# Reordering which activations stay on the chip, when gates and activations are requested, and how gathered rows are spread over the last stages of a layer on Trainium2

## The chip, the cores and the metric

The kernel runs on one core of a Trainium2 chip. The metric is device microseconds of one execution, the median of several runs. Engines are named as in the profile: PE (matrix multiplies; PEld is its weight load), DVE (vector), ACT (scalar), POOL, and SP, which only issues transfers. Transfers are issued from SP, ACT and POOL and run on 16 shared DMA engines. Everything is float32; each matrix product is done as three products of a high and a low part (hi*hi, hi*lo, lo*hi).

## The reference, cut to what matters

One layer for 512 tokens of width 2048: a mixer of two attention-like branches, a cross attention to 256 memory rows, and an expert layer, each followed by a layer norm over a scaled residual. The change lies in the expert layer.

```python
def reference(x, mem, w_in, ...):
    h = hybrid_mixer(x, w_in[l], ...)
    x = layer_norm(DN_ALPHA * x + h, ln_w[l, 0], ln_b[l, 0])
    h = memory_cross_attention(x, mem, w_xq[l], w_xkv[l], w_xo[l])
    x = layer_norm(DN_ALPHA * x + h, ln_w[l, 1], ln_b[l, 1])
    h = peer_ffn(x, peer_wq[l], peer_sub_keys[l], peer_u[l], peer_v[l])
    x = layer_norm(DN_ALPHA * x + h, ln_w[l, 2], ln_b[l, 2])

def peer_ffn(x, w_pq, sub_keys, expert_u, expert_v):   # 8 heads, 128 x 128 = 16384 experts
    q = (x @ w_pq).reshape(B, S, PEER_HEADS, 2, PEER_DK // 2)
    sc = jnp.einsum('bshpd,hpnd->bshpn', q, sub_keys)
    top_s, top_i = lax.top_k(sc, PEER_TOPK)             # 16 of 128, twice per head
    ...                                                  # 16 of the 256 pairs per head
    idx = jnp.take_along_axis(cand_i, best_pos, -1)
    g = jax.nn.softmax(best_s, -1)
    ...                                                  # per block of 128 tokens, 128 experts a token:
        u = expert_u[it]
        a = jnp.einsum('tkd,td->tk', u, xt)
        hact = jax.nn.gelu(a, approximate=False) * gt
        return jnp.einsum('tk,tkd->td', hact, expert_v[it])
```

## The kernel before

**Two ways through the expert layer.** Tokens 0 to 255 (two blocks of 128) fetch the experts that they chose: for each of the 128 choices of a block, one indirect transfer from POOL brings 128 rows of 2048 floats (1 MB, tile `rows`, three buffers) of `peer_u`, later of `peer_v`; DVE takes one pass over each (L1041 a dot product, L1057 a multiply and add). Tokens 256 to 511 use all 16384 experts: U and V are streamed whole, and a table of gates, zero where an expert is not chosen, is multiplied in. The table and the streams are cut by *keys*: key c (0 to 127) is a group of 128 experts.

**How a streamed megabyte is used.** `load_raw` asks for 1 MB on SP's queue (tile `raw`). `shares` has ACT copy it to the high part (L179, two instructions of 128x1024) and DVE subtract to get the low part (L182) in one of two `ring` tiles; PE multiplies from the ring. At each share the function `tick` is called.

**`tick` hands out the gathered rows.** `set_rate(980.0)` makes the rate 256/980 rows a unit for the 256 rows (128 of U, then 128 of V) of token block 1. Each tick adds rate * cost * `state["mult"]` to a credit that is cut at 2.0; each whole credit issues one gather, and DVE's pass over it is put two ticks later. A share of `peer_wq` or V costs 4.0 units, one of U 4.2. `state["mult"]` is set anew for each stage. All 256 must be handed out shortly before the end.

**The stages around the change**, in program order (times are of the trace):

- *Choice* (about 2954 to 3204 us): 16 shares of `peer_wq`, the top-16 search on DVE, and between them 26 calls of `next_a`. `next_a` streams U's next key, has PE compute its activations for 256 tokens (L1301, L1304, L1308, bank `pa`), and, after every second key, ACT apply GELU (L1312) into a tile `ga` of 128x512 (seven buffers, GA = 7).
- *Table* (about 3204 to 3510 us): one-hot rows on DVE (`o1`, `o0`), PE products of them (L1364), copies by ACT to `stage`, eight writes of 2 MB on ACT's queue to `gd` in HBM, and 34 calls of `next_a`.
- *Main loop* (from about 3510 us): eight more calls of `next_a` make 68 keys ahead (LOOK = 68). Then for c0 = 0, 16, ..., 112 (J = 16 keys at a time) two passes over the halves of the output (`stage_o`, dh = 0 and 1), each of eight raws of V, two keys a raw. In pass dh = 0, `stage_h(c)` makes the left factor of a pair of keys: DVE multiplies the activations by the gates (L1401), ACT and DVE split it into `hph` (L147) and `hpl` (L148); the 18 `hp` tiles are nine pairs, eight of which a block of 16 keys needs. Both passes use the same factors. From the second pass of c0 = 48 on, `fill` puts one `next_a` after each raw of V; before that the loop streams V alone.

**What waits in HBM.** The activations of 68 keys don't fit: pairs in `spilled` are written to `gad` on ACT's queue as soon as they are made, and read back as tiles `gb` (three buffers) by `ask_a` on SP's queue. The others keep their `ga` tile until `stage_h` takes it. 28 of 34 pairs are spilled: all but those of keys 0 to 11. Keys run in the order 0, 1, 2, .... Gates come back by `ask_g`, four keys at a time (512 KB, tile `G`, two buffers). `stage_h(c)` asks for the gates of c + 4 (at every fourth key) and for the activations of c + 4.

**The order of the work.** The program is a list; a planner with its own clock decides, before the run, in which order each engine takes its instructions, the earlier in the list first among those it holds to be ready. On the chip each engine keeps that order and waits on semaphores. `after(i, j)` only tells the planner that i stands behind j. `late(i)` is `after(i, state["s"])`: not before the DVE subtraction of the share whose tick came last.

Of the kernel before, what the change touches and what calls it, by code (L numbers as in the profile page):

```python
# [42 lines left out]
J = 16  # L43
GB = 8
LOOK = 68
GA = 7
# [3 lines left out]
def build(tc, I, out):  # L50
    nc = tc.nc
    NC_ = PKEYS
    with ExitStack() as ctx:
# [7 lines left out]
        def nm(s):  # L61
            cnt[0] += 1
            return f"{s}_{cnt[0]}"
# [13 lines left out]
        def pair(pool, tag, bufs, n=512):  # L77
            h = pool.tile([P, n], F32R, tag=tag, bufs=bufs, name=nm(tag + "h"))
            l = pool.tile([P, n], F32R, tag=tag, bufs=bufs, name=nm(tag + "l"))
            return h, l  # L80
# [69 lines left out]
        def load_raw(src, n=2048):  # L150
            raws["n"] += 1
            raws["idle"] = raws["idle"] + 1 if jobs and state["done"] >= len(jobs) else 0
            if raws["idle"] > 6 and raws["n"] % 2:
                raw = rows_tile("raw")
            else:
                p = raws["pools"][raws["n"] % len(raws["pools"])]
                raw = p.tile([P, 2048], F32, tag="raw", bufs=1 if p is raws.get("one") else 2, name=nm("raw"))
            nc.sync.dma_start(raw[:, :n], src)
            return raw
# [129 lines left out]
        gd = dp.tile([P, H // 64, NC_, 64], F32, tag="gd", name="gd")  # L289
        gad = dp.tile([NC_ // 2, P, 2 * H], F32, tag="gad", name="gad")  # L290
# [721 lines left out]
        state = {"done": 0, "credit": 0.0, "rate": 0.0, "later": [], "n": 0, "lag": 3, "mult": 1.0}  # L1012
# [95 lines left out]
        def set_rate(units):  # L1108
            state["rate"] = (len(jobs) - state["done"]) / units
            state["credit"] = 0.0  # L1110
# [22 lines left out]
        for i in range(2):  # L1133
            raw = load_raw(I["memT"][i])
            for q in range(4):
                a, b = pair(mtp, "M", 16)
# [58 lines left out]
        with pool("pick0") as pp:  # L1195
            c = Choice(pp, pp, 1, True)
# [45 lines left out]
        with pool("pick1") as pp:  # L1242
            c = Choice(pp, pp, 1)
# [27 lines left out]
        while state["done"] < len(jobs):  # L1271
# [1 line left out]
        add_jobs(1)  # L1273
        state["lag"] = 2
        set_rate(980.0)
        state["mult"] = 0.5
        xs.close()
        bb.close()

# [1 line left out]
        gas, at = {}, [0]  # L1281

        ahead = [min(NC_, max(LOOK, c + 2 * GA - 2)) for c in range(NC_)]
        spilled = {a // 2 for c in range(NC_) for a in range(ahead[c - 1] if c else 0, ahead[c])
                   if a % 2 and a - c >= 2 * GA - 2}
        abank = [None]

        def next_a(hold=None):

            c = at[0]  # L1290
            at[0] += 1
            if c % 2 == 0:
                abank[0] = ps.tile([P, 512], F32, tag="s2", bufs=2, name=nm("pa"))
            bank = abank[0][:, (c % 2) * H:(c % 2 + 1) * H]
            raw = load_raw(I["uT"][c])
            for uh, ul, o, w in shares(raw, 2.1, hold):
                for kk in range(w // P):
                    k = o // P + kk
                    sl = slice(kk * P, (kk + 1) * P)
                    xh, xl = X2[k]  # L1300
                    i = nc.tensor.matmul(bank, uh[:, sl], xh, start=k == 0, stop=False)  # L1301
                    if k == 0 and c % 2:
                        after(i, abank[1])
                    nc.tensor.matmul(bank, uh[:, sl], xl, start=False, stop=False)  # L1304
                for kk in range(w // P):
                    k = o // P + kk
                    sl = slice(kk * P, (kk + 1) * P)
                    i = nc.tensor.matmul(bank, ul[:, sl], X2[k][0], start=False, stop=k == 15)  # L1308
            abank[1:] = [i]
            if c % 2:  # L1310
                ga = gap.tile([P, 512], F32, tag="ga", bufs=GA, name=nm("ga"))
                nc.scalar.activation(ga, abank[0], AF.Gelu)  # L1312
                if c // 2 in spilled:
                    nc.scalar.dma_start(gad[c // 2], ga)
                else:
                    gas[c // 2] = ga

        raws["pools"], raws["one"] = [wp, rw, wp, rw, gap], gap
        with pool("topk", side="right") as tp:
            c = Choice(pp, tp, 2)  # L1320
# [6 lines left out]
        sel = c.sel  # L1327
        rws.close()
        raws["pools"] = [wp, gap, wp]
        state["mult"] = 1.3  # L1330

        def o_bank():
            return mm_bank()
# [42 lines left out]
        mn = ctx.enter_context(pool("main"))  # L1376
        acc = [mn.tile([P, D], F32, tag=f"acc{t}", name=f"acc{t}") for t in range(HB)]
        hs, g4 = {}, {}
        state["mult"] = 0.925

        def late(i):
            after(i, state["s"])

        def ask_g(c):
            if c < NC_ and c not in g4:
                g4[c] = mn.tile([P, H // 64, 4, 64], F32, tag="G", bufs=2, name=nm("G"))
                late(nc.sync.dma_start(g4[c], gd[:, :, c:c + 4]))

        def ask_a(c):
            if c // 2 in spilled and c // 2 not in gas:  # L1390
                gas[c // 2] = mn.tile([P, 512], F32, tag="gb", bufs=3, name=nm("gb"))
                late(nc.sync.dma_start(gas[c // 2], gad[c // 2]))

        def stage_h(c):
            if c % 4 == 0:
# [12 lines left out]
        def stage_o(c0, dh, fill):  # L1408

            banks = [[o_bank() for g in range(2)] for t in range(HB)]  # L1410
            last = c0 + J == NC_
            for jj in range(J // 2):
                if last and dh and jj == 5:
                    if state["done"] < len(jobs):
                        raise RuntimeError(f"{len(jobs) - state['done']} jobs left")
                    while state["later"]:
                        state["later"].pop(0)[1](state["s"])
                    fin_load()
                raw = load_raw(I["vD"][c0 // 2 + jj, dh])
                for vh, vl, o, w in shares(raw, 2.0):  # L1420
                    for j in range(o // 1024, (o + w) // 1024):
                        c = c0 + 2 * jj + j
                        if dh == 0 and c % 2 == 0:
                            stage_h(c)
                        if c0 == 0 and dh == 0 and c in (10, 12):
                            late(nc.sync.dma_start(acc[c // 2 - 5], x2d[HB + c // 2 - 5].rearrange("p g c -> p (g c)")))
                    js = range(o // 1024, (o + w) // 1024)
                    end = last and dh and jj == J // 2 - 1
                    for ts, low in (((0,), 0), ((0,), 1), ((1,), 0), ((1,), 1)) if end else ((range(HB), 0), (range(HB), 1)):
                        for j in js:  # L1430
                            c = c0 + 2 * jj + j
                            a, b = hs[c]
                            for t in ts:
                                tt = slice(t * P, (t + 1) * P)
                                for g in range(2):
                                    gs_ = slice(j * 1024 - o + g * 512, j * 1024 - o + (g + 1) * 512)
                                    if low:
                                        nc.tensor.matmul(banks[t][g], a[:, tt], vl[:, gs_], start=False,  # L1438
                                                         stop=c == c0 + J - 1)
                                    else:  # L1440
                                        nc.tensor.matmul(banks[t][g], a[:, tt], vh[:, gs_], start=c == c0, stop=False)  # L1441
                                        nc.tensor.matmul(banks[t][g], b[:, tt], vh[:, gs_], start=False, stop=False)  # L1442
                fill(dh * J + 2 * jj + 1)
                if last and dh and jj == J // 2 - 2:
                    fin_gathered(1)
            for t in range(HB):
                for g in range(2):
                    o = acc[t][:, dh * 1024 + g * 512:dh * 1024 + (g + 1) * 512]
                    if c0 == 0:
                        nc.vector.scalar_tensor_tensor(o, o, ALPHA, banks[t][g], op0=ALU.mult, op1=ALU.add)  # L1450
                    else:
                        nc.vector.tensor_add(o, o, banks[t][g])  # L1452
                if last:
                    if t not in fst:
                        fst[t] = mn.tile([P, 32], F32, tag="fst", bufs=2, name=nm("fst"))
                    for g in range(2 * dh, 2 * dh + 2):
                        nc.vector.bn_stats(fst[t][:, 6 * g:6 * g + 6], acc[t][:, g * 512:(g + 1) * 512])
                    if dh:
                        fin(t)
# [19 lines left out]
        for c0 in range(0, NC_, J):  # L1479
            def fill(i, c0=c0):  # L1480
                if i % 2:
                    c = c0 + i // 2
                    while at[0] < (ahead[c + 1] if c + 1 < NC_ else NC_):
                        next_a()
# [82 lines left out]
```

## Time and profile before

| | |
|---|---|
| median of 3 runs | 4677.41 us (4677.14 to 4681.16) |
| the profiled execution's own time | 4678.84 us |
| its span, first to last instruction | 4677.1 us |
| PE, DVE, ACT, POOL busy | 96%, 80%, 48%, 19% of the span |
| moved by DMA | 1488.71 MB, mean 318 GB/s |
| mean granted PE clock | 0.986 |

The profile gives, for a stretch of the run, how long each engine was busy, the share of PE's full clock that was granted, the mean busy share of the 16 DMA engines and what they moved. A wait is told as *who <- whom*: the engine and line that stood idle, and the instruction or transfer that ended the idleness. Matmul ends are modelled, so PE's busy time is an upper bound; waits and the spacing of starts tell more. In the timeline a bracket at the end of a line is the idle time just before it and its releaser.

### The profile page before, as it was taken

How to read it: one execution, taken by the hardware profiler on the slowest of the kernel's cores; microseconds unless marked ns; L12 is line 12 of the kernel's file. 1: busy time of each engine (PE TensorE's matmuls, PEld its weight loads, DVE VectorE, ACT ScalarE, POOL GpSimd, SP SyncE). 2: the span in 40 equal slices, each digit the busy share in tenths (PEclk: the TensorE clock that was granted, in tenths of full speed). 3: DMA queues.
4: the chain of work that ended last, by engine and by line, in shares of the span. 5: the costliest groups of instructions: out<-in, count | busy, mean ns of one | idle time of the engine just before them, and what ended most of it. 6: DMA issues, size and time to landing. Idle time of an engine off the chain costs nothing. (4 is left out here: it accounts for less than half of the span.)

```text
span 4677.1 us, 65189 instructions
## 1 busy us (share of the span) xinstructions
PE 4481.4 (96%) x25662; PEld 3996.6 (85%) x25662; DVE 3750.0 (80%) x4318; ACT 2231.6 (48%) x3037; POOL 888.2 (19%) x631
## 2 busy tenths in 40 slices
PE   8999999999999999999999989999989989999997
PEld 6888888889888899999899767999987778888886
DVE  7877677556898877888778669799878888988888
ACT  6766766654343423333333675435653333433333
POOL 1000000000232222222221000112222322333332
PEclk9999999999999999999999999999999999999999
DMA  7899889666788889888799765667989999999997
GB/s 287 321 335 328 319 324 338 233 217 219 292 339 312 326 330 347 333 332 320 261 350 349 271 223 213 249 260 287 352 353 393 394 371 370 385 371 369 390 368 302
DMA packets 244020, 1488.71 MB, mean 318 GB/s; under 512 B 26588, under 2 KB 52252, under 8 KB 75392
## 3 DMA queue, kind: packets, MB, share of 16 engines
q1 hardware_dynamic: 150384, 888.47, 51.0%
q0 software_dynamic: 81664, 561.95, 31.1%
q10 hardware_dynamic: 11664, 34.12, 1.9%
q8 instruction: 201, 3.29, 0.3%
q14 instruction: 107, 0.88, 0.1%
HBM read 1425.15 MB, written 59.29 MB: 317 GB/s over the span
## 5 line engine op out<-in xcount | busy, mean ns | idle before, releaser
L179 ACT CAST ring<-raw 128x1024 fp32r<-128x1024 f32 x1568 | 1596.4, 1050 | 1486.2 <-PE mm L246 425.6
L182 DVE TENSOR_TENSOR ring<-raw,ring 128x2048 fp32r<-128x2048 f32 (+1 forms) x926 | 1810.6, 1961 | 609.5 <-ACT ring L179 355.5
L1021 POOL DMA_INDIRECT rows<-in_peer_u,ei x256 | 402.1, 1571 | 1660.8 <-DVE rows L1041 786.4
L203 PE MATMUL mm<-Ah,ring 128*128 128x384 f32 x2560 | 672.3, 343 | 14.3 <-ACT Ah L147 8.7
L1041 DVE SCALAR_TENSOR_TENSOR rows<-rows,x2l 128x2048 f32<-128x2048 f32 x256 | 583.3, 2285 | 41.2 <-DMA rows<-in_peer_u,ei 41.2
L1057 DVE SCALAR_TENSOR_TENSOR x2l<-rows,dots,x2l 128x2048 f32<-128x2048 f32 x256 | 600.8, 2347 | 19.3 <-DMA rows<-in_peer_v,ei 17.7
L1021 POOL DMA_INDIRECT rows<-in_peer_v,ei x256 | 419.5, 1639 | 990.0 <-DVE x2l L1057 760.5
L1301 PE MATMUL pa<-Xh,ring 128*128 128x256 f32 x2048 | 502.1, 285 | 22.6 <-ACT ring L179 22.4
L1304 PE MATMUL pa<-Xl,ring 128*128 128x256 f32 x2048 | 498.6, 283 | 0.0
L203 PEld LDWEIGHTS mm<-Ah,ring 128*128 128x128 f32 x2560 | 464.3, 190 | 21.4 <-ACT Ah L147 9.8
L1441 PE MATMUL mm<-ring,hph 128*128 128x512 f32 x1024 | 398.0, 400 | 42.0 <-ACT hph L147 23.9
L203 PE MATMUL mm<-Al,ring 128*128 128x384 f32 x1280 | 429.6, 341 | 1.7 <-DVE Al L148 1.7
L1301 PEld LDWEIGHTS pa<-Xh,ring 128*128 128x128 f32 x2048 | 391.8, 191 | 29.4 <-ACT ring L179 26.6
L1442 PE MATMUL mm<-ring,hpl 128*128 128x512 f32 x1024 | 396.5, 399 | 9.7 <-DVE hpl L148 9.7
L1304 PEld LDWEIGHTS pa<-Xl,ring 128*128 128x128 f32 x2048 | 392.3, 192 | 2.7
L246 PE MATMUL mm<-ring,Zl 128*128 128x512 f32 x832 | 328.2, 394 | 0.0
L245 PE MATMUL mm<-ring,Zh 128*128 128x512 f32 x832 | 327.1, 393 | 0.5 <-ACT ring L179 0.5
L245 PE MATMUL mm<-ring,Ah 128*128 128x512 f32 x768 | 305.7, 398 | 1.1 <-ACT ring L179 1.1
L246 PE MATMUL mm<-ring,Al 128*128 128x512 f32 x768 | 303.2, 395 | 0.0
L1441 PEld LDWEIGHTS mm<-ring,hph 128*128 128x128 f32 x1024 | 194.3, 191 | 90.6 <-ACT hph L147 29.1
L203 PE MATMUL mm<-Bh,ring 128*128 128x384 f32 x1024 | 262.4, 338 | 4.8 <-ACT ring L179 4.1
L1308 PE MATMUL pa<-Xh,ring 128*128 128x256 f32 x2048 | 265.6, 282 | 0.3
(391 smaller groups left out, 7136.3 us busy)
## 6 DMA issues: line engine op xcount, KB each, us to landing
raw<-in_w_in SPq DMA_DIRECT2D x256, 1024.0 KB
raw<-in_uT SPq DMA_DIRECT2D x128, 1024.0 KB
raw<-in_vD SPq DMA_DIRECT2D x128, 1024.0 KB
raw<-in_w_out SPq DMA_DIRECT2D x48, 1024.0 KB
raw<-in_peer_wq SPq DMA_DIRECT2D x48, 1024.0 KB
raw<-in_w_xkv SPq DMA_DIRECT2D x32, 1024.0 KB
raw<-in_w_br_ml SPq DMA_DIRECT2D x32, 1024.0 KB
raw<-in_w_br_fx SPq DMA_DIRECT2D x32, 1024.0 KB
```

Source lines behind the costliest of these rows:

```text
L179: x = nc.scalar.copy(hi[:, c:c + 1024], src[:, c:c + 1024])
L182: s = nc.vector.tensor_sub(lo, src, hi.bitcast(F32))
L203: i = nc.tensor.matmul(o, w, x, start=start and s % per == 0, stop=stop and s % per == per - 1)
L245: nc.tensor.matmul(banks[t], xh[:, tt], wh[:, c], start=k == 0, stop=False)
L246: nc.tensor.matmul(banks[t], xl[:, tt], wh[:, c], start=False, stop=False)
L1021: i = nc.gpsimd.indirect_dma_start(out=rows, out_offset=None, in_=I[table], in_offset=bass.IndirectOffsetOnAxis(ap=ei[t][:, k:k + 1], axis=0))
L1041: i = nc.vector.scalar_tensor_tensor(rows, rows, 1.0, tok[t]["x2l"], op0=ALU.mult, op1=ALU.mult, accum_out=d[:, k % GB:k % GB + 1])
L1057: i = nc.vector.scalar_tensor_tensor(acc, rows, d[:, GB + k % GB:GB + k % GB + 1], acc, op0=ALU.mult, op1=ALU.add)
L1301: i = nc.tensor.matmul(bank, uh[:, sl], xh, start=k == 0, stop=False)
L1304: nc.tensor.matmul(bank, uh[:, sl], xl, start=False, stop=False)
L1441: nc.tensor.matmul(banks[t][g], a[:, tt], vh[:, gs_], start=c == c0, stop=False)
L1442: nc.tensor.matmul(banks[t][g], b[:, tt], vh[:, gs_], start=False, stop=False)
```

## The change

1. The order of U's keys among the 68 ahead becomes `turn_`: 16 to 67, then 0 to 15, then 68 and on. `spilled` is now the pairs of the first 56 keys of that order: the pairs of keys 16 to 67 and of keys 0 to 3. Again 28 pairs; the six that stay on the chip are those of keys 4 to 15, which are computed last.
2. `late` is applied to the requests of gates and activations only for c below 8. From c = 8 on the planner may put a request wherever its tile is free.
3. In pass dh = 1 of every block but the last, after the first and second raw, `ask_g` and `ask_a` are called for the next block (keys c0 + 16 and c0 + 20 of the gates, c0 + 18 and c0 + 20 of the activations). A request that was made already isn't made again.
4. `state["mult"]` goes from 0.5 to 0.65 in the choice, from 1.3 to 1.5 in the table, and from 0.925 to 0.86 in the main loop.

```diff
-        state["mult"] = 0.5
+        state["mult"] = 0.65
...
-        spilled = {a // 2 for c in range(NC_) for a in range(ahead[c - 1] if c else 0, ahead[c])
-                   if a % 2 and a - c >= 2 * GA - 2}
+        turn_ = list(range(J, LOOK)) + list(range(J)) + list(range(LOOK, NC_))
+        spilled = {turn_[a] // 2 for a in range(LOOK - 2 * GA + 2)}
...
-            c = at[0]
+            c = turn_[at[0]]
             at[0] += 1
...
-        state["mult"] = 1.3
+        state["mult"] = 1.5
...
-        state["mult"] = 0.925
+        state["mult"] = 0.86
...
                 g4[c] = mn.tile([P, H // 64, 4, 64], F32, tag="G", bufs=2, name=nm("G"))
-                late(nc.sync.dma_start(g4[c], gd[:, :, c:c + 4]))
+                i = nc.sync.dma_start(g4[c], gd[:, :, c:c + 4])
+                if c < 8:
+                    late(i)
...
                 gas[c // 2] = mn.tile([P, 512], F32, tag="gb", bufs=3, name=nm("gb"))
-                late(nc.sync.dma_start(gas[c // 2], gad[c // 2]))
+                i = nc.sync.dma_start(gas[c // 2], gad[c // 2])
+                if c < 8:
+                    late(i)
...
                 fill(dh * J + 2 * jj + 1)
+                if dh and not last and jj < 2:
+                    ask_g(c0 + J + 4 * jj)
+                    ask_a(c0 + J + 2 + 2 * jj)
```

## Prediction

> **What bounds the kernel now.** The page first. PE is busy nearly throughout, so the question is in which stages it is held up.
>
> ```profile
> PE 4481.4 (96%) x25662; PEld 3996.6 (85%) x25662; DVE 3750.0 (80%) x4318; ACT 2231.6 (48%) x3037; POOL 888.2 (19%) x631
> ```
>
> Second, busy times by stretch. The columns are the stretch, its length, busy time of PE, PEld, DVE, ACT and POOL (instructions in brackets), granted clock, DMA share, GB/s. The first four rows are choice with table, choice, table, and a stall inside the table; then come six passes over V alone, dh = 1 of c0 = 0 up to dh = 0 of c0 = 48, and their sum; last the part that streams U and V.
>
> ```profile
> 2954.00:3510.00 556.00, 516.35 (x4218) 511.87 (x4219) 487.03 (x867) 293.98 (x594) 108.92 (x65) 0.96 0.79 301
> 2954.00:3204.00 250.00, 235.53 (x1924) 232.97 (x1925) 226.29 (x590) 98.24 (x111) 35.62 (x22) 0.97 0.67 254
> 3204.00:3510.00 306.00, 280.82 (x2297) 278.90 (x2296) 260.75 (x279) 195.75 (x484) 73.29 (x43) 0.96 0.88 340
> 3477.00:3486.00 9.00, 0.24 (x3) 0.03 (x1) 0.00 (x0) 1.19 (x2) 0.20 (x1) 0.72 1.02 428
> 3590.00:3636.00 46.00, 45.69 (x199) 36.67 (x197) 38.38 (x32) 18.19 (x20) 14.76 (x7) 1.00 0.92 372
> 3636.00:3694.00 58.00, 48.70 (x192) 37.36 (x191) 49.86 (x47) 21.30 (x26) 15.63 (x10) 0.94 1.02 415
> 3694.00:3737.00 43.00, 43.00 (x188) 34.88 (x187) 37.09 (x31) 17.13 (x18) 15.91 (x8) 1.00 0.91 352
> 3737.00:3797.00 60.00, 50.55 (x193) 38.88 (x192) 50.62 (x45) 19.64 (x23) 16.85 (x9) 0.91 0.94 369
> 3797.00:3841.00 44.00, 44.00 (x192) 35.76 (x191) 37.83 (x30) 16.48 (x20) 12.48 (x7) 1.00 0.95 371
> 3841.00:3894.00 53.00, 46.00 (x188) 35.53 (x187) 46.64 (x42) 19.38 (x24) 11.95 (x8) 0.97 1.02 409
> 3590.00:3894.00 304.00, 277.94 (x1144) 219.09 (x1143) 260.42 (x225) 112.11 (x127) 87.58 (x49) 0.97 0.96 383
> 3894.00:4594.00 700.00, 682.50 (x4360) 618.59 (x4359) 606.08 (x340) 273.27 (x305) 230.25 (x121) 1.00 0.95 374
> ```
>
> Both kinds of pass have eight raws of V and some 190 matmuls; the ones with dh = 1 take 46, 43 and 44 us with PE always busy, those with dh = 0 take 58, 60 and 53. The 38 us between are lost where the left factors are made. In the U-and-V part PE is at 97.5% and there is little to win.
>
> Third, what PE waited for: two rows of the V-alone part (3510 to 3894 us), one of the table, one of the U-and-V part.
>
> ```profile
> PE mm L1441 <- ACT hph L147: 23.9, 10, 5.3
> PE mm L1442 <- DVE hpl L148: 8.1, 6, 2.6
> PE pa L1301 <- ACT ring L179: 11.7, 3, 9.3
> PE mm L1441 <- ACT ring L179: 17.2, 12, 1.6
> ```
>
> In the V-alone part 32.0 us go to late left factors. In the table one stall of 9.3 us stands out. The timeline shows both: first ACT and PE in the table, then SP, DVE and PE around the start of the pass c0 = 32, dh = 0.
>
> ```profile
> 3453.04 0.81 ACTq L1371 DMA_DIRECT2D gd<-stage  x2
> 3456.57 0.33 ACTq L1314 DMA_DIRECT2D gad<-ga  x1
> 3469.46 2.00 ACT L179 CAST ring<-raw 128x1024 fp32r<-128x1024 f32 x2 [7.83 <-DMA raw<-in_uT]
> 3484.34 0.60 ACT L1312 ACTIVATE ga<-pa 128x512 f32<-128x512 f32 x1 [12.88 <-DMA gad<-ga]
> 3485.41 3.88 ACT L179 CAST ring<-raw 128x1024 fp32r<-128x1024 f32 x4 [0.48 <-ACT ga L1312]
> 3487.32 0.41 PE L1304 MATMUL pa<-Xl,ring 128*128 128x256 f32 x1
> 3497.11 0.28 PE L1304 MATMUL pa<-Xl,ring 128*128 128x256 f32 x1
> ...
> 3729.36 0.53 SPq L1387 DMA_DIRECT2D G<-gd  x1
> 3729.94 0.61 SPq L1392 DMA_DIRECT2D gb<-gad  x1
> 3752.61 0.69 DVE L1401 TENSOR_TENSOR gb<-gb,G 128x512 f32<-128x512 f32 x1
> 3754.00 1.22 PE L1441 MATMUL mm<-ring,hph 128*128 128x512 f32 x2 [4.58 <-ACT hph L147]
> ```
>
> **The table's stall, part 1 of the change.** Keys 0 to 11 run first and hold six of the seven `ga` tiles until the main loop, so 28 pairs pass through the seventh, each waiting for the write before it. The write issued at 3456.57 stands behind two of 2 MB, and ACT waits 12.88 us; the casts for PE wait behind it. With the kept keys last, all seven tiles rotate and no GELU waits for a write. PE's 9.3 us don't all go: ACT had waited 7.83 us for a raw just before, while the DMA engines were full (1.02), and the two raws cast at 3485.41 landed somewhere between 3469 and 3485. Taken at the middle, 3478, the first cast is done at 3479 and some 2.5 us of stall remain. After the stall PE ran slow: starts 0.21 us apart instead of 0.12 from 3486.5 to 3491.2, which costs 4.7 * (1 - 0.12/0.21), about 2 us. Bounds 0 (the raws were the limit) and -11.4; I take **-8**. Nothing is added: 28 writes and 28 reads as before. Keys 0 to 3 must now be read back at the start, keys 12 to 15 no longer: two loads of 256 KB moved from the middle of the first pass to its start. If they land late they cost up to the longest wait of this kind, 5.3; where they leave, as much may go. I take 0.
>
> **The requests, parts 2 and 3.** Keys c0 + 0 and c0 + 2 of a block already get their left factors a pass ahead. For c0 = 32 the gates and activations of key 36 are asked for at 3729.36 and 3729.94, 8 us before the pass begins at 3737; DVE's multiply comes at 3752.61 and PE stands 4.58 us. DVE did not stand idle for it: the planner put it there, because it held the data for late. The new calls ask for just these (c0 + 20) during the pass dh = 1 before, and without `late` the rest follow as tiles come free, so the planner can put multiplies and splits between the shares of dh = 1, as the `hp` pairs come free there. The most that can be won: PE's floor is six passes at 43 us, 258 of 304. The DMA engines set a nearer one. 304 us at 383 GB/s are 116.4 MB; part 4 takes 4 rows or 4.2 MB away; 112.2 MB at 415 GB/s, the best pass, are 270.5 us, so -33.5. The other end is 0. Half of it, **-17**: the full rate was held only in single passes. By the Trainium skill, page DMA: Bandwidth & Descriptors, section Bandwidth, transfers between HBM and SBUF are bound at about 358 GB/s for a core; then only the 4.2 MB would count here, -11.7 by estimate, and the sum would be 5 us smaller. The pass at 415 GB/s speaks against that bound.
>
> What a free request costs: SP is one queue, and a request whose tile is not free holds up the raws behind it. These are SP's own waits in the V-alone part.
>
> ```profile
> SPq L158 <- DVE ring L182: 253.1, 57, 11.0
> SPq L1392 <- DVE hpl L148: 36.9, 14, 6.0
> SPq L1387 <- DVE gb L1401: 12.1, 4, 4.7
> ```
>
> Of the requests of `gb` and G there, 18 already make SP stand, 49.0 us in all, 2.7 each. PE has no row of waiting for a raw there, so I take 0 and price the other end as a rival.
>
> **The rows, part 4.** By the credit rule: rate 256/980 = 0.2612. Choice: 0.52 to 0.55 a tick before, 0.68 to 0.71 after, over 42 ticks 22 and 29 rows. Table: 1.43 a tick, cut at 2.0, gives 2, 1, 1 in turn, 46 over 34 ticks; 1.65 gives 2, 1, 2, 1 and 51. Three in turn is what three `rows` buffers hold. The main loop has 188, then 176: four fewer in the six V-alone passes, eight in the U-and-V part. The last row is handed out at the same share of V in both, so the end doesn't move. One row is 1 MB and on DVE this (U rows; the accumulator's read follows each):
>
> ```profile
> L1041 DVE SCALAR_TENSOR_TENSOR rows<-rows,x2l x42: 2278/2286/2293, 3220.7 to 3507.3; 128x2048 f32<-128x2048 f32 x42
> L1041 DVE DVE_READ_ACCUMULATOR rows<-rows,x2l x42: 75/83/89, 3222.9 to 3509.6; 128x1 f32 x42
> DVE rows L1041 <- DMA rows<-in_peer_u,ei: 25.7, 10, 5.1
> DVE v L904 <- ACT sc L999: 19.2, 5, 10.5
> DVE ring L182 <- ACT ring L179: 18.3, 7, 11.4
> DVE o L1357 <- PE mm L1364: 9.0, 7, 2.8
> ```
>
> 12 rows are 12 * 2.37 = 28.4 us more of DVE in choice and table; POOL's issues, and DMA at 0.79 of the stretch, have room. DVE has 487.0 of 556 us there; after it 515.5 of what the table's gain leaves, 556 - 11.4 at most = 544.6, or 94.7%, more than in any stage now. The last four rows are DVE's waits there, 72.2 us; 11.4 of them belong to the table's stall. Were the other 60.8 to stay, the two stages would take 515.5 + 60.8 = 576.3, which is +31.7. The other end is 0, since 29 us of idle remain. Rows and scores (25.7 and 19.2) land at their own time, so a later DVE waits less for them; only 15.9 are steps of chains with ACT and PE. That is nearer the low end; I take a third, **+10**. In the main loop the 4 rows are in the term above; the U-and-V part loses 8 MB and 19 us of DVE, but PE waits there for ACT's casts alone, 17.2 in all: **-2**, between 0 and -17.
>
> **Sum.** -8 - 17 + 10 - 2 = -17. On the profiled execution's 4678.84 us that is 4662; its median of three runs is 4677.41, 1.4 less, so the forecast is **4660 us**. About 0.2%, 9.4 us, is what can be told from no change.
>
> **Rivals.**
> - *The requests do nothing.* The multiply at 3752.61 is late although its data was asked for 23 us before; if the planner's order comes from DVE being full, asking earlier changes nothing. Then the 17 us go: 4677. Against it: keys 32 and 34, asked for a pass before, are not late.
> - *DVE becomes the bound in choice and table.* The term of +10 is its full +31.7: -8 - 17 + 31.7 - 2, so +5, 4682. For it: 94.7%. Against: PE has no wait for DVE in the choice now.
> - *SP stands (the slower one).* The 30 requests of gates and 26 of activations from c = 8 on are no longer tied to a share. At 2.7 us each they would hold SP 152 us. If a fifth of that reaches PE as late raws, 30 us, and the 17 are lost, 4707. It decides from 13 us, 8% of the 152. For it: the DMA engines leave the raws little lead. Against: raws too wait on DVE (253.1 us), which releases both in its order.
> - *All of it comes.* -11.4 for the table, -33.5 for the passes, -5 in the first pass, -2, and no cost on DVE: -52, 4625. Then DVE has to run the first two stages at 95% without holding PE.
>
> **How the numbers follow.** Forecast 0.42 (its own range 4645 to 4672), requests do nothing 0.15, DVE the bound 0.17, SP stands 0.13, all of it 0.13. Faster by over 0.2%: most of the forecast, all of the last, and the lucky ends of the second and third, 0.60. Within 0.2%: the rest of those, 0.25. Slower: SP, and the bad end of DVE, 0.15. The range leaves out SP's case and the far ends: 4628 to 4686.
>
> **What would show it.** Right: no GELU waits for a write to `gad`; passes with dh = 0 of c0 = 16, 32 and 48 take under 52 us, and PE's 32.0 us of waiting for `hph` and `hpl` fall to half; requests of G and `gb` stand between the raws of dh = 1. Wrong: choice and table together over 556 us, with PE waiting for DVE's low parts (L1308 <- L182); SP's waits at L1387 and L1392 well over 49 us with PE waiting for casts that wait for raws.

## The result, and the profile after

The changed kernel takes **4648.64 us** (4643.34 to 4651.7) against 4677.59 us (4677.14 to 4681.16) for the kernel before: a ratio of 0.9935, 95% interval 0.9918 to 0.9952, faster by 29 us. The forecast was 4660, in a range of 4628 to 4686.

The same stretches as in the prediction, now of the changed kernel (stretch, length, busy PE, PEld, DVE, ACT, POOL, granted clock, DMA share, GB/s): choice with table, choice, table; the first pass; the six V-alone passes and their sum; the U-and-V part.

```profile
2956.00:3510.00 554.00, 520.27 (x4261) 514.14 (x4262) 505.20 (x883) 298.71 (x598) 128.29 (x72) 0.98 0.82 321
2956.00:3212.00 256.00, 240.90 (x1955) 238.47 (x1956) 240.66 (x599) 98.85 (x112) 48.95 (x29) 0.97 0.73 286
3212.00:3510.00 298.00, 279.37 (x2309) 275.67 (x2308) 264.55 (x285) 199.87 (x486) 79.34 (x43) 0.99 0.90 351
3528.00:3583.00 55.00, 47.33 (x201) 37.57 (x200) 47.14 (x44) 23.17 (x29) 9.43 (x9) 0.97 1.01 405
3583.00:3635.00 52.00, 47.72 (x196) 37.06 (x195) 46.06 (x42) 19.84 (x24) 8.33 (x8) 0.97 1.01 410
3635.00:3680.00 45.00, 44.16 (x191) 35.22 (x190) 40.82 (x34) 16.68 (x18) 11.55 (x8) 1.00 1.01 406
3680.00:3726.00 46.00, 45.66 (x197) 36.19 (x196) 44.67 (x39) 19.72 (x24) 8.29 (x8) 1.00 1.00 404
3726.00:3774.00 48.00, 44.84 (x191) 35.02 (x190) 41.34 (x36) 17.16 (x19) 10.86 (x9) 1.00 1.01 407
3774.00:3820.00 46.00, 45.66 (x197) 36.20 (x196) 44.84 (x41) 19.91 (x24) 7.93 (x7) 1.00 1.00 402
3820.00:3866.00 46.00, 45.01 (x193) 35.48 (x192) 41.62 (x33) 16.84 (x18) 14.93 (x9) 1.00 1.00 395
3583.00:3866.00 283.00, 273.04 (x1156) 215.16 (x1155) 259.35 (x220) 110.14 (x126) 61.90 (x48) 0.99 1.01 404
3866.00:4564.00 698.00, 679.55 (x4349) 617.16 (x4349) 591.23 (x331) 276.64 (x305) 260.25 (x115) 1.00 0.93 369
```

The sawtooth of 46, 58, 43, 60, 44, 53 us has become 52, 45, 46, 48, 46, 46, and the DMA engines, which swung between 352 and 415 GB/s, move 395 to 410 in every pass. In the kernel before, the loads of gates and activations for a block are asked for in its pass dh = 0 and in the last 8 us ahead of it; now nine of the twelve for c0 = 32 are asked for in the pass dh = 1 before and three in dh = 0.

PE's waits in these six passes, and SP's own:

```profile
PE mm L1445 <- ACT ring L179: 5.2, 3, 2.1
PE mm L1442 <- DVE ring L182: 3.1, 5, 0.8
PE mm L1445 <- DVE acc L1457: 1.1, 1, 1.1
PE mm L1445 <- DVE acc L1459: 0.4, 2, 0.2
...
SPq L158 <- DVE ring L182: 150.7, 42, 8.1
SPq L1394 <- DVE hpl L148: 39.2, 21, 5.0
SPq L1387 <- DVE gb L1405: 27.7, 12, 3.0
```

No wait for `hph` or `hpl` is left. DVE's timeline shows why. Its multiplies by the gates now stand spread over the pass dh = 1 of c0 = 0, five of them, where before two stood there, both at its start. Changed kernel first, then the kernel before:

```profile
3592.01 0.68 DVE L1405 TENSOR_TENSOR gb<-gb,G 128x512 f32<-128x512 f32 x1
3608.93 0.69 DVE L1405 TENSOR_TENSOR gb<-gb,G 128x512 f32<-128x512 f32 x1
3616.66 0.69 DVE L1405 TENSOR_TENSOR gb<-gb,G 128x512 f32<-128x512 f32 x1
3622.36 0.69 DVE L1405 TENSOR_TENSOR gb<-gb,G 128x512 f32<-128x512 f32 x1
3627.98 0.69 DVE L1405 TENSOR_TENSOR gb<-gb,G 128x512 f32<-128x512 f32 x1
...
3591.10 0.68 DVE L1401 TENSOR_TENSOR gb<-gb,G 128x512 f32<-128x512 f32 x1
3595.10 0.69 DVE L1401 TENSOR_TENSOR gb<-gb,G 128x512 f32<-128x512 f32 x1 [0.92 <-DMA gb<-gad]
```

**Where the 29 us come from.** Stage lengths in us, from the first start of L1301 (choice), of L1364 (table), of the first product with V (first pass), and of the first of DVE's adds at the end of a pass; the last stage runs to the end of the kernel. All kernels of the experiments are in it, each from its profiled execution.

| kernel | choice | table | first pass | six V-alone | U-and-V to end | sum |
|---|---|---|---|---|---|---|
| before | 255.3 | 317.1 | 58.2 | 305.7 | 781.0 | 1717.3 |
| changed | 260.7 | 309.3 | 51.2 | 282.4 | 780.3 | 1683.9 |
| e1 order only | 255.0 | 309.7 | 50.3 | 307.2 | 779.3 | 1701.5 |
| e2 requests only | 255.7 | 316.4 | 55.1 | 283.0 | 775.4 | 1685.6 |
| e3 rows only | 260.6 | 323.5 | 52.9 | 303.3 | 764.1 | 1704.4 |
| e4 order and requests | 253.9 | 306.1 | 49.8 | 284.8 | 785.0 | 1679.6 |
| e5 late lifted only | 255.1 | 315.7 | 56.1 | 278.4 | 775.6 | 1680.9 |
| e6 early calls only | 254.7 | 316.4 | 59.0 | 301.3 | 790.0 | 1721.4 |
| e7 changed, GELU behind | 260.0 | 310.4 | 49.0 | 291.8 | 760.8 | 1672.0 |
| e8 changed, rows shifted | 259.9 | 308.1 | 50.5 | 277.4 | 792.3 | 1688.2 |
| e9 before, GELU behind | 255.1 | 312.8 | 58.7 | 305.7 | 770.8 | 1703.1 |
| e10 e3, GELU behind | 260.7 | 323.0 | 53.4 | 302.7 | 760.3 | 1700.1 |
| e11 e4, GELU behind | 256.4 | 307.5 | 46.8 | 291.6 | 767.8 | 1670.1 |
| e12 e7, fewer in choice | 255.9 | 310.2 | 51.1 | 280.1 | 768.7 | 1666.0 |

Each row is one execution, so how far can a stage be trusted? Some kernels have the same order of instructions on every engine in a stage, and still differ there. In the six passes the changed kernel and e7 take 282.4 and 291.8 us, e4 and e11 284.8 and 291.6; where the passes are held up, before and e9 take 305.7 both. In choice and first pass such pairs differ by up to 3.0 us, in the table by 4.3 (before and e9, but for two neighbours on ACT that changed places). The groups stand clear of that: with the rows of before the table takes 306.1 to 309.7 us in the new order and 312.8 to 317.1 in the old one; the six passes take 277.4 to 291.8 with the ties lifted and 301.3 to 307.2 without; the choice takes 259.9 to 260.7 with 0.65 and 253.9 to 256.4 with 0.5.

The theory (A) was that the parts act in separate stages: the order in the table, the requests in the passes, the rows as a cost in choice and table. Rivals: the order or the smaller number of rows made the passes faster.

### The profile page after: what moved, and what is told of

It reads as the page before. It is cut to its first block, busy times and chain, and to the rows that moved or that the text cites. A ratio compares the mean times of both kernels' runs of the same rounds, so it can differ in the third digit from the quotient of the medians.

```text
span 4645.8 us, 65087 instructions
## 1 busy us (share of the span) xinstructions
PE 4473.6 (96%) x25662; PEld 3989.6 (86%) x25662; DVE 3743.1 (81%) x4318; ACT 2231.4 (48%) x3037; POOL 906.6 (20%) x631
## 4 chain that ended last, share of the span: by engine, by line
PE 59%; DVE 6%; DMA 5%; issue 4%; ACT 2%; POOL 1%; ACTq 0%; DVEq 0%; SPq 0%; POOLq 0%
PE mm L203 19%; PE mm L253 5%; PE mm L245 5%; PE mm L246 5%; PE mm L1445 4%; PE mm L1446 4%; PE mm L1442 4%; PE pa L1308 4%; PE pa L1301 3%; PE pa L1304 3%; DVE ring L182 3%; ACT ring L179 1%; DVE rows L1041 1%; DMA raw<-in_vD 1%; PE sm L684 1%
## 5 line engine op out<-in xcount | busy, mean ns | idle before, releaser
L1021 POOL DMA_INDIRECT rows<-in_peer_u,ei x256 | 376.6, 1471 | 1635.0 <-DVE rows L1041 787.0
L1021 POOL DMA_INDIRECT rows<-in_peer_v,ei x256 | 463.4, 1810 | 967.8 <-DVE x2l L1057 677.8
L1301 PE MATMUL pa<-Xh,ring 128*128 128x256 f32 x2048 | 499.1, 285 | 17.7 <-ACT ring L179 17.6
L1301 PEld LDWEIGHTS pa<-Xh,ring 128*128 128x128 f32 x2048 | 390.0, 190 | 23.4 <-ACT ring L179 21.1
```

The costliest lines, as they stand in the source:

```text
L1021: i = nc.gpsimd.indirect_dma_start(out=rows, out_offset=None, in_=I[table], in_offset=bass.IndirectOffsetOnAxis(ap=ei[t][:, k:k + 1], axis=0))
```

## The experiments

Each ratio is against the kernel before.

**e1: the order alone** (the diff's `turn_` and `spilled`).

> Part 1 alone (order of U's keys and which activations stay), rows and requests as before. Theory A (the table's stall came from writes queueing for the one free tile; the requests, not the order, made the passes faster): no GELU waits for a write to gad, the stall of 9.3 us at the end of the table shrinks to about 3, the table is 6 to 10 us shorter, the six V-alone passes stay within 3 us of their 305 us; total -6 to -12 us. Rival B (the raws were late anyway, and the order freed the passes): table within 2 us of before, V-alone passes shorter by 10 us or more.

Measured: 4661.12 us, ratio 0.9958 [0.9941, 0.9974]. No wait of a GELU for a write to `gad` is left; in the table PE now waits for casts as in this row, against 11.7 us with a longest of 9.3 before:

```profile
PE pa L1301 <- ACT ring L179: 3.7, 2, 2.7
```

The table is 7.4 us shorter and the six passes are 1.5 us longer: A. Not expected: the first pass is 7.9 us shorter.

**e2: the requests alone** (parts 2 and 3).

> Parts 2 and 3 alone (requests freed of late and asked a pass ahead), order and rows as before. Theory A: choice and table as before within 3 us, stall of about 9 us still in the table; V-alone passes with dh = 0 fall from 58-60 to about 48 us and those with dh = 1 rise from 43-46 to about 47, PE's waits for hph and hpl in them under 5 us; six passes 285 to 290 us (4.2 MB more than the changed kernel at 404 GB/s is 10 us more at most); total -15 to -25 us. Rival C (the four rows taken from the passes did it): passes within 5 us of before, total within 6 us.

Measured: 4650.38 us, 0.9944 [0.9925, 0.9963]: almost the whole gain. Six passes 283.0, table as before. So the passes became faster without fewer rows. The U-and-V part is 5.6 us shorter, which A did not foresee.

**e3: the rows alone.**

> Part 4 alone (more rows beside choice and table, fewer in the main loop). Theory A: choice 4 to 7 us longer, table 0 to 8 us longer, V-alone passes 0 to 6 us shorter because their left factors, not the DMA engines, hold them; total 0 to +10 us. Rival C: passes 10 us shorter or more, total -5 to -10 us.

Measured: 4666.88 us, 0.9972 [0.9962, 0.9982]: faster, so A's total was wrong. Its stages were right: choice +5.3, table +6.4, six passes -2.4. In the table the stall has grown, from 12.88 us on ACT to 20.84:

```profile
3498.80 0.60 ACT L1312 ACTIVATE ga<-pa 128x512 f32<-128x512 f32 x1 [20.84 <-DMA gad<-ga]
```

But the U-and-V part is 16.9 us shorter.

**e4: order and requests, the rows of before.**

> Parts 1 to 3, the rows of before. If the parts add up: choice as before, table 8 to 12 us shorter, V-alone passes 285 to 292 us, total -20 to -35 us, within 8 us of the changed kernel on either side. If the rows are what the rest needs (the passes bound by the DMA engines once requests are free): total 8 us or more above the changed kernel. If the rows only cost (DVE in the choice): 5 us or more below it.

Measured: 4650.25 us, 0.994 [0.9923, 0.9957], as the changed kernel. The rows neither carry the rest nor cost anything that the totals show.

**e5 and e6: which of the two request edits.** e5 only lifts `late` from key 8 on, e6 only adds the calls in dh = 1 and keeps the ties.

> Part 2 alone (requests from key 8 on no longer tied to a share), order, rows and early calls as before. Theory A1 (the ties were what kept the left factors late): the six V-alone passes fall from 306 to about 285 us and PE's waits for hph and hpl in them from 32 us to under 8. Theory A2 (the request one pass ahead is needed, since the planner puts stage_h's requests no earlier than its own place): six passes 298 us or more, waits for hph and hpl 20 us or more.

> Part 3 alone (gates and activations of the next block's keys 4 and 5 pairs in asked after the first and second raw of dh = 1, but still tied to the share of the moment). A1: only the first late factor of each block goes (the 4.6 us wait at the start of c0 = 32 and its like), six passes 295 to 302 us. A2: six passes about 285 us.

Measured: e5 4649.26 us, 0.9941 [0.9923, 0.9959], six passes 278.4; e6 4683.31 us, 1.0014 [1.0004, 1.0024], six passes 301.3. PE's waits in the six passes, the kernel before first, then e5, then e6:

```profile
PE mm L1441 <- ACT hph L147: 15.9, 8, 4.6
PE mm L1442 <- DVE hpl L148: 8.1, 6, 2.6
...
PE mm L1442 <- DVE ring L182: 4.8, 5, 2.0
PE mm L1445 <- ACT ring L179: 4.6, 5, 1.6
...
PE mm L1441 <- ACT hph L147: 17.3, 8, 4.2
PE mm L1442 <- DVE hpl L148: 4.2, 4, 1.4
```

A1: the tie was what kept the left factors late. A request asked for early but tied to a share changes little; e6 as a whole is even 5.5 us slower. And e5 runs the instructions of every engine in the order of e2, which has the calls too, over the whole kernel (but for two neighbours on ACT). With the ties lifted, the new calls change nothing.

**e7: GELU's place in ACT's order.** In the changed kernel's U-and-V part PE waits for ACT's cast 10 times, 16.2 us; e3 has 2 such waits, 3.2 us. In the timeline such a wait follows a GELU that ends ACT's waiting for PE, with the cast that PE needs next behind it. One of them, in the kernel before:

```profile
4010.27 0.60 ACT L1312 ACTIVATE ga<-pa 128x512 f32<-128x512 f32 x1 [6.17 <-PE pa L1308]
4010.77 3.88 ACT L179 CAST ring<-raw 128x1024 fp32r<-128x1024 f32 x4
4011.86 0.50 PE L1441 MATMUL mm<-ring,hph 128*128 128x512 f32 x1 [1.62 <-ACT ring L179]
```

The edit ties the GELU behind the casts of the next share:

```diff
+                if ring.get("gelu") is not None:      # in shares, after the casts (x is the last)
+                    after(ring["gelu"], x)
+                    ring["gelu"] = None
...
-                nc.scalar.activation(ga, abank[0], AF.Gelu)
+                i = nc.scalar.activation(ga, abank[0], AF.Gelu)
+                if at[0] > LOOK:
+                    ring["gelu"] = i
```

> The changed kernel, and in the part that streams U and V the GELU of a pair of keys is ordered behind ACT's casts of the next share of V. Theory D (PE's waits of 1.6 us there come from a GELU that stands in ACT's order ahead of the cast that PE needs next, and how many there are, 3 to 11 a run, is the planner's luck): no such wait is left, the U-and-V part shrinks by 15 to 20 us, the rest as in the changed kernel; total 4628 to 4636 us. Rival: the DMA engines (0.93 busy there) take the place; waits for raws appear, total within 5 us of the changed kernel.

Measured: 4626.0 us, 0.9891 [0.9867, 0.9916], faster than both kernels. All that PE waited for in the U-and-V part, changed kernel first, then e7:

```profile
PE mm L1445 <- ACT ring L179: 16.2, 10, 1.6
PE pa L1308 <- DVE ring L182: 1.9, 6, 0.3
PE mm L1442 <- DVE ring L182: 0.4, 1, 0.4
...
PE pa L1311 <- DVE ring L185: 1.9, 6, 0.3
PE mm L1447 <- DVE ring L185: 0.4, 1, 0.4
```

The stage is 19.5 us shorter: theory D. The six passes are 9.4 us longer here, but not by the edit: no engine's order of instructions differs there from the changed kernel's. The first of the six took 57.2 us at 380 GB/s and a granted clock of 0.91 in e7's profile, 51.5 us at 410 GB/s and 0.97 in the changed kernel's.

**e8: are the freed passes bound by the DMA engines?** `state["mult"]` is 0.7 in the main loop and 0.93 from c0 = 48, dh = 1 on.

> The changed kernel with the main loop's multiplier at 0.70 while V is streamed alone and 0.93 from the second pass of c0 = 48 on: 35 gathered rows in the six V-alone passes in place of 43, 129 in place of 118 after. Theory E (once the requests are free these passes are bound by the DMA engines at about 404 GB/s): 8.4 MB less are 20.8 us at that rate, down to PE's floor of 43 to 44 us a pass, so the six passes go from 282 to 263 to 270 us, PE's waits for casts there vanish; the U-and-V part grows by 0 to 8 us. Rival F (left factors or DVE hold the passes): six passes within 5 us of 282.

Measured: 4656.09 us, 0.9958 [0.9944, 0.9971]. Six passes 277.4, 5 us less; U-and-V to the end 12 us longer. The eight rows (8.4 MB) of the expectation did not all leave: the trace has 42 gathers in these passes against 48, and 277.4 us at 397 GB/s are 4 MB less than 282.4 us at 404. The first of the six and the last two:

```profile
3579.00:3631.00 52.00, 47.45 (x195) 36.87 (x194) 45.48 (x42) 21.38 (x26) 8.35 (x8) 0.97 1.01 410
3769.00:3813.00 44.00, 44.00 (x193) 35.73 (x191) 39.90 (x35) 19.76 (x23) 7.85 (x7) 1.00 0.96 384
3813.00:3857.00 44.00, 44.00 (x192) 35.79 (x191) 35.84 (x29) 18.14 (x19) 9.77 (x7) 1.00 0.96 376
```

By the totals E is missed and F just met, but 5 us is less than the same order of instructions varies by here, so the single passes must decide. The last two reach PE's floor, with the DMA engines at 0.96, and were only some 2 us above it in the changed kernel. The first of the six, with the reads for the next block now in it, stays at 52 us with the DMA engines full. So E holds for that pass, and in the last ones there was little left to free.

**e9, e10, e11: the rows again, without GELU's luck.** e7's edit on the kernel before, on e3, and on e4.

> The kernel before, with only the GELU of the U-and-V part ordered behind the next share's casts. Theory D: PE's 17 us of waits for casts there go, the part shrinks by 15 to 20 us, choice, table and passes as before; total -14 to -22 us. Rival: the planner puts another instruction in its place, total within 5 us.

> Part 4 alone (more rows beside choice and table) on the kernel with the GELU so ordered. Theory G (part 4 alone was faster by luck of GELU's place; by itself it costs DVE time in choice and table): 0 to +8 us against the kernel before with GELU so ordered, choice 5 longer, table 0 to 6 longer, passes 0 to 8 shorter, U-and-V within 3. Rival H (eight rows fewer do speed the U-and-V part): -8 us or more, U-and-V 8 us shorter or more.

> Parts 1 to 3 with the rows of before, GELU so ordered. Against the changed kernel with GELU so ordered (4626): Theory G: 4618 to 4628, choice 5 us shorter, six passes 0 to 8 longer. Rival H: 4634 or more, U-and-V part longer by 8 or more.

Measured: e9 4671.23 us, 0.9978 [0.9967, 0.9989]; e10 4662.89, 0.9974 [0.9963, 0.9984]; e11 4633.13, 0.9898 [0.9881, 0.9916]. On the old kernel the edit is worth 10.2 us in its stage, half of what D forecast; from 3900 to 4540 us PE's waits for casts fall from 15.6 to 4.4 us. e9 to e10, the rows cost 5.6 us in the choice and 10.2 in the table and give back 5.3 in the first pass, 3.0 in the six and 10.5 after. e11 to e7, they cost 3.6, 2.9 and 2.2 us in the first three stages and give 7.0 after. The intervals overlap in both pairs. G falls as stated, for it had the U-and-V part within 3 us. H's conditions are met in e10 (8.3 us less in all, 10.5 in that part) and missed by 1 us in e11 (4633.13, 7.0).

But the last column holds two things: PE's work up to its last product, and a tail in which DVE ends the last gathered rows and the layer norms. Split at the end of that product (us):

| kernel | PE's part | its waits for casts | tail |
|---|---|---|---|
| before | 759.9 | 17.2 | 21.1 |
| changed | 759.2 | 16.2 | 21.1 |
| e2 | 749.5 | 11.3 | 25.9 |
| e3 | 745.6 | 3.2 | 18.5 |
| e4 | 756.7 | 14.6 | 28.3 |
| e7 | 739.8 | 0.0 | 21.1 |
| e9 | 749.8 | 7.8 | 21.1 |
| e10 | 741.7 | 0.0 | 18.5 |
| e11 | 739.6 | 0.0 | 28.3 |
| e12 | 742.7 | 0.2 | 25.9 |

From e11 to e7 PE's part stays, and the 7 us are the tail: in e4, whose tail is as long as e11's, a row's pass and the statistics of the gathered tokens stand behind DVE's last adds (4616.73 us), in the changed kernel ahead of them. From e9 to e10, 7.8 of the 8.1 us of PE's part are waits for casts that e9 still had; whether fewer rows or the planner's order ended those is not shown. So H's reason, that fewer rows speed PE's work, is not borne out by e11 and e7; the rows also move the place of the last gathered row, and with it the tail. Of e3's 16.9 us, 14.0 are waits for casts and 2.6 the tail.

**e12: a better split.** e7 with 0.5 in the choice and 0.91 from c0 = 48, dh = 1 on.

> The changed kernel with GELU so ordered, multiplier 0.5 in the choice (22 rows in place of 29) and 0.91 from the second pass of c0 = 48 on (125 in place of 118). Theory G: choice 5 us shorter, U-and-V 0 to 3 longer as PE is held by nothing there; total 4618 to 4625. Rival H: U-and-V longer by 5 or more, total 4626 or more.

Measured: 4627.03 us, 0.9889 [0.9872, 0.9905], level with e7. The choice is 4.1 us shorter, the end 7.9 longer, 4.8 of it the tail. Both are as H stated; 3.0 us of the end are PE's part.

## Why the prediction was right, and where its sizes were off

**The table's stall, -8.** Right: e1's table is 7.4 us shorter, by the named cause, and no GELU waits for `gad`. In the changed kernel the table is 7.8 us shorter; e4, with the rows of before, has -11.0.

**The requests, -17.** Right in place and in the tie, too small: -23.3 in the changed kernel. "Half of" the bound was the mis-sized step: the reason given, that the full rate was held only in single passes, did not hold, since once the reads are spread 404 GB/s are held over all six. Its bound of 270.5 us was not passed by any kernel. One thing was wrong inside it: the prediction gave the new calls as what brings the left factors forward and the lifted ties as what lets the rest follow. e6 shows that the calls alone bring 4.4 us in the passes and leave the whole 5.5 us longer; e5 shows that the lifted ties bring everything.

**SP's queue, 0.** Nearly right. SP's waits at requests in the six passes rose from 48.8 us in 17 to 66.9 us in 33. PE's waits for casts there rose from none to 5.2 us, and ACT's waits for raws from 37.9 to 72.6; whether the queue or the full DMA engines did that is not shown. 5.2 us is the most that it cost.

**The first pass, 0.** Wrong by 7 us, beyond the bound of 5.3 either way. PE's two waits for `hph` in that pass, 8.0 us, are gone, but 7.7 us of waits for casts have come. Part of the 7 us lies in where the stage begins and ends: in the kernel before some 17 of U's products, about 2 us at 0.12 us each, still run behind V's first. That the loads for keys 12 to 15 left the pass is true; that this made the gain is not shown, since e3 has -5.3 there with the old order.

**The rows, +10.** e4 to the changed kernel, choice +6.8 and table +3.2, is +10.0; e3 alone has +11.7. That it meets the forecast is partly luck. The credit rule gave 12 more rows in the two stages; the traces have 8 more gathers, 30 against 23 in the choice and 46 against 45 in the table, and DVE is busy 18.2 us longer there, not 28.4. And +3.2 in the table is within what the same order varies by; the +6.4 of e3 is the grown stall. The cost in the choice is real, but PE does not pay it as waits for DVE's low parts (0.6 us). DVE, at 240.66 of 256 us, ends the search 5.5 us later, counted from the stage's start, and PE stands 6.35 us before the table's first product, 3.44 before. The rival that all of DVE's waits stay (+31.7) fell.

**U-and-V, -2.** -0.7 in the changed kernel, and the tail is 21.1 us in both, as the prediction said of the end. Here the prediction read the row (17.2 us of waiting for casts) but took it as unaffected. It is decided by where the planner puts the GELU, and most edits redraw that: 11.3 us in e2, 3.2 in e3, 16.2 with all parts. That the changed kernel's draw was like that of before is luck; with e3's, the same change would have come out some 13 us faster. The stage and the first pass, which e1, e2 and e3 each shorten, are the main reasons why the parts alone (15.8, 31.7 and 12.9 us by the last column) add to 60 and together give 33.4.

**The bound of 358 GB/s.** The bound of about 358 GB/s that the Trainium skill gives on the page DMA: Bandwidth & Descriptors, section Bandwidth, is there the share of a core when both cores of the HBM domain stream, which the prediction left out. This kernel, on one core, held 404 GB/s over 283 us.

Still open: what makes the freed passes take 282.4 us in one execution and 291.8 in another, with the same instructions in the same order.

## What to carry to other kernels

When an engine waits for an operand whose inputs were asked for in time, look at what the planner knew: a tie that only orders a request can keep everything that hangs on it behind. A buffer set that is kept long should be filled last, so that the passing tiles have all buffers. And before a part of a change is credited with a gain in a stage that it doesn't touch, see whether two instructions on an in-order engine there have merely changed places, and whether the tail behind the last product has moved.

## What the runs showed of the hardware that was not expected

The part before the choice is the same code in all fourteen profiled kernels, yet the choice began between 2952.2 us (e10) and 2967.1 us (e6): a spread of 15 us, half of what the change is worth. The six freed passes, with the same order on every engine, took 282.4 us at 404 GB/s in one profile and 291.8 us at 396 GB/s in another; the passes held up by late left factors took 305.7 us twice. Lengths of stages separate causes here that totals of a few runs would blur, but only where they differ by more than the same order of instructions does.
